# RMS norm on one core: three loads moved to ScalarE's DMA queue, the last tile's halves swapped

## Chip, core and metric

The kernel runs on one core of one Trainium2 chip. The metric is device time in microseconds (us), the median of several runs. One further execution was taken with the hardware profiler; all rows and instants below come from it, counted from the start of its span. A "unit" below is half a tile, 4096 KB of data.

## What is computed

The input x has 16 x 1024 rows of 512 float32 numbers. Each row is divided by its root mean square and multiplied by a vector gamma of 512 numbers:

```python
rms = np.sqrt(np.mean(x ** 2, axis=-1, keepdims=True) + 1e-5)
return (x / rms * gamma).astype(np.float32)
```

33.6 MB are read and 33.6 MB written. Nothing is reused between rows but gamma.

## The kernel before

The 16384 rows are four tiles of 4096. In a tile each of the 128 partitions holds 32 whole rows, so half a tile (16 rows per partition) is 32 KB per partition and 4096 KB in all. On the chip there are three buffers, `slots[0]` to `slots[2]` (line 40), each of one tile. Tiles 0, 1 and 2 have a slot each; tile 3 reuses slot 0 (`slot_of`, line 86), so its loads must wait until tile 0 has been stored. Rows 23 to 31 of slot 2 also serve as scratch for tile 0's squares (line 90), so that part of tile 2 can't be loaded before VectorE has read those squares.

The work goes group by group, a group being half a tile (`groups`, lines 76 to 85: tile, first row, number of rows, the pieces in which the squares are taken, and how many rows GpSimd scales). For a group:

- `square_sums` (line 88): ScalarE squares a piece (line 95), VectorE sums it by row (line 96). Pieces alternate between one PSUM buffer of 7 rows and one SBUF buffer of 5 rows, so a third piece waits until VectorE has read the first.
- `inverse_rms` (line 100): ScalarE's square root (line 101), VectorE's reciprocal (line 102).
- GpSimd scales its share of the rows and multiplies them by gamma (lines 108, 109). ScalarE scales the others, one instruction per row (line 117), and VectorE multiplies them by gamma (line 121).

The loop at line 161 is a software pipeline: in the turn of one group ScalarE squares the next group's first two pieces, scales the first half of its rows of this group, squares the third piece, and scales the second half. Every engine executes its own instructions in the order written; nothing reorders them (`manual_schedule`, line 33).

All DMAs are issued by SyncE (SP) and stand in one queue, q1. SP issues in the order written and waits, before an issue, for what that transfer depends on. The order is: tile 0 in three loads with gamma between them, both halves of tile 1, and then what `transfers` (line 128) adds: both halves of tile 2, both stores of tile 0, both loads of tile 3 (each waits until the store of the same rows has landed), one store of the whole of tile 1, one of tile 2, and two stores of tile 3, first half first. SP issues the last store when VectorE has done line 121 of the last group.

In the text below, L2b is the load of tile 2's second half, S0a the store of tile 0's first half, and so on; L1 and S1 are of a whole tile.

Of the kernel before, what the change touches and what calls it, by code (L numbers as in the profile page):

```python
# [9 lines left out]
def kernel(  # L10
# [6 lines left out]
    nc = tc.nc  # L17
# [12 lines left out]
    xv = xf.rearrange("(t p r) d -> t p r d", p=P, r=R)  # L30
# [9 lines left out]
    slots = [const.tile([P, R, D], fp32, name=f"slot{i}") for i in range(3)]  # L40

    before_scale = []

    def load(t, slot, r0, r1):
        dma = nc.sync.dma_start(out=slots[slot][:, r0:r1], in_=xv[t][:, r0:r1])  # L45
        before_scale.append((slot, r0, r1, dma))

    def store(t, slot, r0, r1):
        dma = nc.sync.dma_start(out=ov[t][:, r0:r1], in_=slots[slot][:, r0:r1])
        before_scale.append((slot, r0, r1, dma))  # L50

    gamma_row = const.tile([1, D], fp32)
    pieces = (0, D)

    load(0, 0, 0, 1)
    load(0, 0, 1, 16)
    for c0, c1 in zip(pieces, pieces[1:]):
        nc.sync.dma_start(out=gamma_row[:, c0:c1], in_=gamma.unsqueeze(0)[:, c0:c1])
    load(0, 0, 16, 32)
    load(1, 1, 0, 16)  # L60
    load(1, 1, 16, 32)

    ones_col = const.tile([1, P], fp32)
    nc.gpsimd.memset(ones_col, 1.0)  # L64
# [15 lines left out]
        (1, 16, 16, (7, 5, 4), 7),  # L80
        (2, 0, 16, (7, 5, 4), 7),
        (2, 16, 16, (7, 5, 4), 7),
        (3, 0, 16, (7, 5, 4), 7),
        (3, 16, 16, (7, 5, 4), 3),
    ]
    slot_of = [0, 1, 2, 0]

    def square_sums(ss, t, g, r, m, k):
        if m == 9:
            sq = slots[2][:, 23:32, :]  # L90
        else:
            home, name, most = ((psum, "sq_psum", 7), (const, "sq_sbuf", 5))[k % 2]
            sq = home.tile([P, most, D], fp32, name=name)
        rows = slots[slot_of[t]][:, g + r : g + r + m, :]
        nc.scalar.activation(out=sq[:, :m], in_=rows, func=AF.Square)  # L95
        nc.vector.tensor_reduce(  # L96
            out=ss[:, r : r + m, 0], in_=sq[:, :m], axis=mybir.AxisListType.X, op=OP.add
        )

    def inverse_rms(ss, n):  # L100
        nc.scalar.activation(out=ss[:, :n, 0], in_=ss[:, :n, 0], func=AF.Sqrt, bias=eps_t, scale=1.0 / D)  # L101
        nc.vector.reciprocal(out=ss[:, :n, 0], in_=ss[:, :n, 0])  # L102
        return ss

    def scale_by_pool(rstd, t, g, n, share):
        part = slots[slot_of[t]][:, g + n - share : g + n, :]
        by_row = rstd[:, n - share : n].to_broadcast([P, share, D])
        nc.gpsimd.tensor_tensor(out=part, in0=part, in1=by_row, op=OP.mult)  # L108
        last = nc.gpsimd.tensor_tensor(  # L109
            out=part, in0=part, in1=gamma_b.to_broadcast([P, share, D]), op=OP.mult  # L110
        )
        before_scale.append((slot_of[t], g + n - share, g + n, last))

    def scale(rstd, t, g, r0, r1):
        x = slots[slot_of[t]]
        for r in range(r0, r1):
            nc.scalar.activation(out=x[:, g + r, :], in_=x[:, g + r, :], func=AF.Copy, scale=rstd[:, r])  # L117

    def times_gamma(t, g, r0, r1):
        part = slots[slot_of[t]][:, g + r0 : g + r1, :]  # L120
        scaled = nc.vector.tensor_tensor(  # L121
            out=part, in0=part, in1=gamma_psum.to_broadcast([P, r1 - r0, D]), op=OP.mult
        )
        for slot, b0, b1, earlier in before_scale:
            if slot == slot_of[t] and b0 < g + r1 and g + r0 < b1:
                tc.declare_no_dep(scaled.ins, earlier.ins, reason="ScalarE waited for it before it scaled these rows")

    def transfers(t, g):
        if (t, g) == (0, 0):
            load(2, 2, 0, 16)  # L130
            load(2, 2, 16, 32)
        elif (t, g) == (0, 16):
            store(0, 0, 0, 16)
            store(0, 0, 16, 32)
            load(3, 0, 0, 16)
            load(3, 0, 16, 32)
        elif (t, g) == (1, 16):
            store(1, 1, 0, 32)
        elif (t, g) == (2, 16):
            store(2, 2, 0, 32)  # L140
        elif (t, g) == (3, 0):
            store(3, 0, 0, 16)
        elif (t, g) == (3, 16):
            store(3, 0, 16, 32)

    def pieces_of(group):
        t, g, n, pieces, share = group
        ss = stats.tile([P, 16, 1], fp32, name="ss")
        r = 0
        todo = []  # L150
        for k, m in enumerate(pieces):
            todo.append((ss, t, g, r, m, k))
            r += m
        return ss, todo
# [6 lines left out]
    for k, group in enumerate(groups):  # L161
        t, g, n, pieces, share = group
        mine = n - share
        half = (mine + 1) // 2
        ahead = groups[k + 1 :][:1]
        ss, todo = pieces_of(ahead[0]) if ahead else (None, [])
        scale_by_pool(rstd, t, g, n, share)
        for piece in todo[:2]:
            square_sums(*piece)
        scale(rstd, t, g, 0, half)  # L170
        for piece in todo[2:]:
            square_sums(*piece)
        scale(rstd, t, g, half, mine)
        times_gamma(t, g, 0, mine)
        transfers(t, g)
        for nxt in ahead:
            rstd = inverse_rms(ss, nxt[2])

# [29 lines left out]
```

## Time and profile before

| what | us |
|---|---|
| median of 3 runs (161.77 to 162.13) | 161.85 |
| the profiled execution's own time | 161.72 |
| its span | 159.9 |
| VectorE (DVE) busy | 112.8 |
| ScalarE (ACT) busy | 109.1 |
| GpSimd (POOL) busy | 102.1 |
| DMA queue q1, share of 16 engines' span | 98.1% |

The span begins with the first instruction and ends with the last. The rows show when an instruction started and how long it took, and for a DMA the time from its issue to its landing, which is when its semaphore is complete. A DMA's issue instant plus its time to landing gives the instant from which others may use the data. The queue takes transfers in order, so the time to landing holds the time that a transfer stood behind others.

### The profile page before, as it was taken

The page shows a single profiled execution, that of the slowest core. Times are in us where ns is not written, and L with a number is a line of the kernel's source. Part 1 is how long each engine was busy: PE and PEld are TensorE (multiplying, and loading weights), DVE is VectorE, ACT ScalarE, POOL GpSimd, SP SyncE. Part 2 cuts the span into 40 slices and gives each one's busy share as a digit, 9 for nine tenths or more (in the row PEclk, how much of TensorE's full clock was granted, in tenths as well). Part 3 has the DMA queues.
Part 4 walks back from the last instruction along what each step waited for, and adds up shares of the span by engine and source line. Part 5 has one row for each costly group of instructions (what it writes and reads, how often), then busy time and mean ns, then how long its engine had stood idle before and what let it go on. Part 6 is the DMA issues. An engine that isn't in the chain of part 4 may idle for free.

```text
span 159.9 us, 258 instructions
## 1 busy us (share of the span) xinstructions
PE 2.0 (1%) x2; PEld 0.5 (0%) x2; DVE 112.8 (71%) x38; ACT 109.1 (68%) x110; POOL 102.1 (64%) x22
## 2 busy tenths in 40 slices
PE   0005000000000000000000000000000000000000
PEld 0001000000000000000000000000000000000000
DVE  0000993797999999999999999999999702950000
ACT  3007906999998899899989989999994297000000
POOL 1000005994079999999999999999999997000000
DMA  5989999999999997999999999997997998999995
GB/s 191 492 369 468 451 393 434 484 393 418 484 410 393 483 426 311 483 393 402 508 402 393 492 426 393 524 475 311 524 459 328 524 426 361 393 459 459 393 426 229
DMA packets 2163, 67.12 MB, mean 420 GB/s; under 512 B 241, under 2 KB 241, under 8 KB 370
## 3 DMA queue, kind: packets, MB, share of 16 engines
q1 hardware_dynamic: 2162, 67.11, 98.1%
q14 instruction: 1, 0.01, 0.0%
HBM read 33.56 MB, written 33.55 MB: 420 GB/s over the span
## 4 chain that ended last, share of the span: by engine, by line
DVE 62%; ACT 18%; DMA 7%; ACTq 0%; SPq 0%; issue 0%
DVE ss L96 36%; DVE slot L121 26%; ACT slot L117 9%; DMA slot<-in_x_dram 7%; ACT slot L95 5%; ACT sq_psum L95 4%; DVE ss L102 1%; ACTq L203 0%; ACT gamma_b L160 0%; SPq L45 0%; ACT ss L101 0%; ACTq L95 0%
## 5 line engine op out<-in xcount | busy, mean ns | idle before, releaser
L108 POOL TENSOR_TENSOR slot<-slot,ss 128x3584 f32<-128x3584 f32 (+2 forms) x8 | 45.0, 5625 | 31.8 <-DVE ss L102 31.8
L96 DVE TENSOR_REDUCE ss<-sq_psum 128x7 f32<-128x3584 f32 (+1 forms) x14 | 44.5, 3176 | 19.5 <-ACT sq_psum L95 19.5
L109 POOL TENSOR_TENSOR slot<-slot,gamma_b 128x3584 f32<-128x3584 f32 (+2 forms) x8 | 56.9, 7112 | 0.6
L117 ACT ACTIVATE slot<-slot,ss 128x512 f32<-128x512 f32 x77 | 48.5, 707 | 4.9 <-DVE ss L102 4.9
L121 DVE TENSOR_TENSOR slot<-slot,gamma_psum 128x4608 f32<-128x4608 f32 (+2 forms) x8 | 42.3, 5282 | 9.3 <-ACT slot L117 9.3
L95 ACT ACTIVATE sq_psum<-slot 128x3584 f32<-128x3584 f32 (+1 forms) x14 | 36.5, 2604 | 11.4 <-DMA slot<-in_x_dram 10.4
L96 DVE TENSOR_REDUCE ss<-sq_sbuf 128x5 f32<-128x2560 f32 x6 | 16.8, 2806 | 0.0
L95 ACT ACTIVATE sq_sbuf<-slot 128x2560 f32<-128x2560 f32 x6 | 13.9, 2320 | 0.0
L96 DVE TENSOR_REDUCE ss<-slot 128x9 f32<-128x4608 f32 x2 | 9.9, 4953 | 0.1
L101 ACT ACTIVATE ss<-ss,eps_t 128x16 f32<-128x16 f32 x8 | 2.4, 306 | 8.4 <-DVE ss L96 8.4
L95 ACT ACTIVATE slot<-slot 128x4608 f32<-128x4608 f32 x2 | 8.1, 4028 | 0.0
L102 DVE RECIPROCAL ss<-ss 128x16 f32<-128x16 f32 x8 | 2.0, 249 | 0.4 <-ACT ss L101 0.4
L66 PE MATMUL gamma_psum<-gamma_row,ones_col 1*128 1x512 f32 x2 | 2.0, 1120 | 12.8 <-DMA gamma_row<-in_gamma_dram 12.8
L72 ACT ACT_TABLE_LOAD x1 | 1.3, 1283 | 1.1 <-PEq L192 1.1
L160 ACT COPY gamma_b<-gamma_psum 128x512 f32<-128x512 f32 x1 | 0.6, 566 | 0.0
L66 PEld LDWEIGHTS gamma_psum<-gamma_row,ones_col 1*128 1x128 f32 x2 | 0.5, 304 | 12.8 <-issue 12.8
L64 POOL MEMSET ones_col<- 1x128 f32 x1 | 0.2, 194 | 0.3 <-POOLq L192 0.3
L192 POOL MEMSET const-float32-0.0<- 128x1 f32 x1 | 0.1, 98 | 0.2 <-issue 0.2
L72 ACT ACTIVATE table<-eps_t 128x1 f32<-128x1 f32 x1 | 0.2, 203 | 0.0
L192 POOL MEMSET const-bfloat16-1.0<- 128x1 bf16 x1 | 0.1, 101 | 0.0
L192 POOL MEMSET const-uint8-127<- 128x1 uint8 x1 | 0.1, 101 | 0.0
L192 POOL MEMSET const-float32-1.0<- 128x1 f32 x1 | 0.1, 98 | 0.0
(1 smaller groups left out, 0.1 us busy)
## 6 DMA issues: line engine op xcount, KB each, us to landing
slot<-in_x_dram SPq DMA_DIRECT2D x7, 4096.0 KB, 27.1
out_dram<-slot SPq DMA_DIRECT2D x4, 4096.0 KB, 21.8
slot<-in_x_dram SPq DMA_DIRECT2D x1, 3840.0 KB, 11.8
slot<-in_x_dram SPq DMA_DIRECT2D x1, 256.0 KB, 3.1
out_dram<-slot SPq DMA_DIRECT2D x2, 29.2
gamma_row<-in_gamma_dram SPq DMA_DIRECT2D x1, 2.0 KB
```

The costliest lines, as they stand in the source:

```text
L66: nc.tensor.matmul(gamma_psum[:, 0], ones_col, gamma_row, start=True, stop=True)
L72: nc.scalar.activation(out=table, in_=eps_t, func=AF.Sqrt)
L95: nc.scalar.activation(out=sq[:, :m], in_=rows, func=AF.Square)
L96: nc.vector.tensor_reduce(out=ss[:, r : r + m, 0], in_=sq[:, :m], axis=mybir.AxisListType.X, op=OP.add)
L101: nc.scalar.activation(out=ss[:, :n, 0], in_=ss[:, :n, 0], func=AF.Sqrt, bias=eps_t, scale=1.0 / D)
L102: nc.vector.reciprocal(out=ss[:, :n, 0], in_=ss[:, :n, 0])
L108: nc.gpsimd.tensor_tensor(out=part, in0=part, in1=by_row, op=OP.mult)
L109: last = nc.gpsimd.tensor_tensor(out=part, in0=part, in1=gamma_b.to_broadcast([P, share, D]), op=OP.mult)
L117: nc.scalar.activation(out=x[:, g + r, :], in_=x[:, g + r, :], func=AF.Copy, scale=rstd[:, r])
L121: scaled = nc.vector.tensor_tensor(out=part, in0=part, in1=gamma_psum.to_broadcast([P, r1 - r0, D]), op=OP.mult)
L160: nc.scalar.copy(out=gamma_b[:, 0], in_=gamma_psum[:, 0])
L192: nc = _bacc.Bacc("TRN2", target_bir_lowering=False, num_devices=1)
```

## The change

Transfers only; every computing instruction stays, and on VectorE, GpSimd and TensorE the order and the shapes stay too. On ScalarE three DMA issues are put between the computing instructions.

1. L1 becomes one load of 8192 KB (before: two of 4096 KB). L2a follows at once.
2. L2b, L3b and L3a are issued by ScalarE, on a queue of its own: L2b in the turn of group (0, 16) after the first scaling; L3b in the turn of (1, 16) after the third piece of squares; L3a in the turn of (2, 0) after the first two pieces of squares.
3. The last two groups change places: (3, 16) with GpSimd's share 7 comes first, (3, 0) with share 3 last.
4. S0b is issued before S0a. S1 becomes S1a and S1b, and S1a is made to wait until L3b has landed. S3b is issued before S3a.

```diff
-    load(1, 1, 0, 16)
-    load(1, 1, 16, 32)
+    load(1, 1, 0, 32)
+    load(2, 2, 0, 16)
...
-        (3, 0, 16, (7, 5, 4), 7),
-        (3, 16, 16, (7, 5, 4), 3),
+        (3, 16, 16, (7, 5, 4), 7),
+        (3, 0, 16, (7, 5, 4), 3),
...
-    def transfers(t, g):
-        if (t, g) == (0, 0):
-            load(2, 2, 0, 16)
-            load(2, 2, 16, 32)
-        elif (t, g) == (0, 16):
+    late = {}
+
+    def loads_amid(t, g, step):
+        if (t, g, step) == (0, 16, 1):
+            load(2, 2, 16, 32, queue=nc.scalar)
+        elif (t, g, step) == (1, 16, 2):
+            late[3] = load(3, 0, 16, 32, queue=nc.scalar)
+        elif (t, g, step) == (2, 0, 0):
+            load(3, 0, 0, 16, queue=nc.scalar)
+
+    def stores(t, g):
+        if (t, g) == (0, 16):
+            store(0, 0, 16, 32)
             store(0, 0, 0, 16)
-            store(0, 0, 16, 32)
-            load(3, 0, 0, 16)
-            load(3, 0, 16, 32)
         elif (t, g) == (1, 16):
-            store(1, 1, 0, 32)
+            store(1, 1, 0, 16, behind=late[3])
+            store(1, 1, 16, 32)
         elif (t, g) == (2, 16):
             store(2, 2, 0, 32)
-        elif (t, g) == (3, 0):
-            store(3, 0, 0, 16)
-        elif (t, g) == (3, 16):
-            store(3, 0, 16, 32)
+        elif t == 3:
+            store(3, 0, g, g + 16)
...
         for piece in todo[:2]:
             square_sums(*piece)
+        loads_amid(t, g, 0)
         scale(rstd, t, g, 0, half)
+        loads_amid(t, g, 1)
         for piece in todo[2:]:
             square_sums(*piece)
+        loads_amid(t, g, 2)
         scale(rstd, t, g, half, mine)
         times_gamma(t, g, 0, mine)
-        transfers(t, g)
+        stores(t, g)
```

`load` takes the queue as an argument; `store` takes `behind`, a load whose landing the issue waits for.

More of the change, by code (lines that the diff above doesn't have):

```diff
@@ L42, with load, store @@
     before_scale = []
-    def load(t, slot, r0, r1):
-        dma = nc.sync.dma_start(out=slots[slot][:, r0:r1], in_=xv[t][:, r0:r1])
+    def load(t, slot, r0, r1, queue=nc.sync):
+        dma = queue.dma_start(out=slots[slot][:, r0:r1], in_=xv[t][:, r0:r1])
         before_scale.append((slot, r0, r1, dma))
-    def store(t, slot, r0, r1):
+        return dma
+    def store(t, slot, r0, r1, behind=None):
         dma = nc.sync.dma_start(out=ov[t][:, r0:r1], in_=slots[slot][:, r0:r1])
+        if behind is not None:
+            tc.add_manual_dep(
+                dma.ins,
+                behind.ins.name,
+                mybir.DependencyInfo(mybir.DependencyClass.Sync, mybir.DependencyReason.DATA),
+                reason="the store is issued when this load has landed",
+            )
         before_scale.append((slot, r0, r1, dma))
```

## Prediction

> **What bounds the kernel now.** I read the busy shares first, then the DMA queue, then the chain of waits, then the last rows of the timeline. From the page:
>
> ```profile
> DMA  5989999999999997999999999997997998999995
> GB/s 191 492 369 468 451 393 434 484 393 418 484 410 393 483 426 311 483 393 402 508 402 393 492 426 393 524 475 311 524 459 328 524 426 361 393 459 459 393 426 229
> ...
> q1 hardware_dynamic: 2162, 67.11, 98.1%
> ...
> DVE 62%; ACT 18%; DMA 7%; ACTq 0%; SPq 0%; issue 0%
> ```
>
> The chain says VectorE, and misleads: it starts from the last computing instruction and leaves out the DMA behind it. That instruction is the second row here, from the timeline; the first is the last store's issue, from SyncE's timeline:
>
> ```profile
> 142.22 0.33 SPq L49 DMA_DIRECT2D out_dram<-slot  x1
> ...
> 135.06 7.09 DVE L121 TENSOR_TENSOR slot<-slot,gamma_psum 128x6656 f32<-128x6656 f32 x1 [8.13 <-ACT slot L117]
> ```
>
> VectorE ends at 142.15, the span at 159.9. Between them lies only storing, and the last store takes 16.9 us from issue to landing though a unit (4096 KB) needs 9.7: it stood behind S3a. These are the DMA issues, each asked for in a short window: L2a (issued at 3.40), L2b (38.01), L3b (81.97), S1 (86.93), S3b (142.22):
>
> ```profile
> slot<-in_x_dram SPq DMA_DIRECT2D x1, 4096.0 KB, 48.4
> ...
> slot<-in_x_dram SPq DMA_DIRECT2D x1, 4096.0 KB, 24.2
> ...
> slot<-in_x_dram SPq DMA_DIRECT2D x1, 4096.0 KB, 19.1
> ...
> out_dram<-slot SPq DMA_DIRECT2D x1, 33.5
> ...
> out_dram<-slot SPq DMA_DIRECT2D x1, 4096.0 KB, 16.9
> ```
>
> Issue plus time gives landings. The loads issued at 1.17, 2.02, 2.40, 2.89, 3.40 and 38.01 landed at 12.97, 22.7, 32.4, 42.1, 51.8 and 62.2: **9.7 us a unit**, but 10.4 for the last. L3b landed at 101.1, S1 (two units) at 120.4, S3b at 159.1. From 12.97 fifteen units follow: 12.97 + 15 x 9.71 = 158.6. So in the whole run the queue lost 0.5 us, all of it around 60 us, where loads hand over to stores. The windows say the same: 434 GB/s where only loads run, 320 in the 4 us around the handover, 431 where only stores run:
>
> ```profile
> 13.00:42.00 29.00, 1.88 (x2) 0.30 (x2) 20.79 (x6) 23.93 (x18) 12.01 (x2) 1.00 1.01 434
> ...
> 60.00:64.00 4.00, 0.00 (x0) 0.00 (x0) 4.00 (x2) 3.91 (x5) 4.00 (x1) 1.00 0.75 320
> ...
> 144.00:158.00 14.00, 0.00 (x0) 0.00 (x0) 0.00 (x0) 0.00 (x0) 0.00 (x0) 1.00 1.00 431
> ```
>
> The kernel is bound by the bytes that 16 DMA engines move. The change moves the same bytes. It can win at most the 0.6 us at the handover, unless two queues together run faster than one; it can lose by leaving the engines dry or by making them alternate.
>
> **SyncE's waits taken away: 0.** SyncE stood 22.2 us in front of L3a and L3b, waiting for S0a and S0b to land. Behind it stood only S1, whose data were ready at 86.93, and the engines were busy throughout.
>
> **L1 in one load.** Its semaphore now comes with the whole tile, at 42.1. ScalarE's next squares ran from 39.23 on, since L1a had landed at 32.4. The rows that move:
>
> ```profile
> 39.23 3.14 ACT L95 ACTIVATE sq_psum<-slot 128x3584 f32<-128x3584 f32 x1
> ...
> 44.72 3.83 DVE L96 TENSOR_REDUCE ss<-sq_psum 128x7 f32<-128x3584 f32 x1
> ...
> 48.58 1.88 ACT L95 ACTIVATE sq_psum<-slot 128x2048 f32<-128x2048 f32 x1 [0.57 <-DVE ss L96]
> ...
> 53.38 4.95 DVE L121 TENSOR_TENSOR slot<-slot,gamma_psum 128x4608 f32<-128x4608 f32 x1
> ```
>
> ScalarE: 42.2 + 3.14 + 2.32 (second piece) + 3.17 (five scalings) = 50.8, then L2b's issue. Such a row exists on SyncE only, 0.33 to 0.47; I take 0.35 (bounds 0 and 0.5): 51.1. Third piece to 53.0, four scalings to 55.5. Line 121 starts at 55.5 instead of 53.38: VectorE's chain is **2.1 us late**, and stays so, as VectorE has no idle time from 39 to 127. GpSimd's next share waits for the reciprocal, 60.4 instead of 58.88, thus 1.5 late. The two later issues cost nothing: ScalarE idles 0.56 per turn at line 101.
>
> What covers this: the last store would be issued at 142.22 + 2.1 = 144.3, while S3b holds the engines until about 149.0. A first byte follows an issue by 0.8 to 1.3 us (the first issue is at 0.74, the first bytes are in the slice 1.5 to 2.0). So 3.4 us or more of cover are left, and the direct price is 0. With no cover it would be 2.1.
>
> **First handover to stores.** SyncE now issues S0b first, which needs line 121 of group (0, 16): ready at 58.33 before, at 60.4 after. S0a, ready at 44.7, stands behind it. Meanwhile only L2b feeds the engines, on ScalarE's queue: issued at 50.8, in time, as L2a lands at 51.8. Without a handover L2b would land at 51.8 + 9.7 = 61.5, its last bytes some 0.4 earlier (L0's bytes end and landing stand about so). S0b's first bytes come at 60.4 + 0.8 to 1.3 = 61.2 to 61.7. Gap: 0.1 to 0.6, and the old loss of 0.6 may be gone (the queue is another) or come on top. Against the 0.6 of before: -0.5 to +0.6. I take +0.1, a gap of 0.35 with half of the old loss.
>
> The Trainium skill, "DMA: Bandwidth & Descriptors", section "Latency and other measured facts", gives about 0.6 us to the first byte for queues of SyncE and ScalarE. By it this gap would be 0 and the sum 0.3 lower; the row here, 0.8 or more, is longer, and I go by the row.
>
> **Second handover, S0a to L3b.** ScalarE reaches L3b's issue at 77.8 + 2.1 = 79.9, first bytes at 80.7 to 81.2. S0b and S0a, begun at 61.5, end at 61.5 + 19.4 = 80.9. Gap 0 to 0.3; I take 0.1. The issue itself waits for S0b, landed by about 72; nothing waits on ScalarE. L3a's issue at 88.5 waits for S0a, landed by 82.
>
> **Two queues at once.** L3b lands at about 91.2, only then is S1a issued, with S1b behind it. L3a has been running since 90.8 on the other queue. From 92.4 both have work: 6.6/8 of a unit of L3a is left, and if both get half, the mixed stretch lasts 2 x 0.83 x 9.7 = 16 us, to 108.5. No row shows two queues. Nearest rows: loads alone and stores alone run at 434 and 431 GB/s, so a mean of them costs 0; a handover inside one queue cost 0.6 once and 0 once (L3b to S1: 120.4 - 101.1 = 19.3 for two units of 9.7). A unit is 128 blocks of 32 KB (one per partition) for 16 engines, eight each; seven changes at 0.6 would be 4 us. The lower end: the window 100 to 120 shows 462 GB/s, 6% over, though its neighbour 419, since large packets are counted at their end; 6% of 16 us would be -1.0. I take +0.2, near the row of 0.
>
> L3a lands at about 109.0 (needed by the squares of group (3, 0) at 108.46 + 2.1 = 110.6). The margin is 1.6 us.
>
> That both get half is supported by the same page, section "Queues, rings and completion order", which says that each engine goes round-robin between queues, packet by packet. By it L3a is in time; no row of this trace can show it.
>
> **The rest.** S1a and S1b end with L3a's bytes at 90.8 + 3 x 9.7 = 119.9; S2, issued at 114.93 + 1.5 = 116.4, follows without a gap; S3b is ready at 128.9 + 1.5 = 130.4, S2's bytes last to 139.3. Swapping the halves of tile 3 changes no duration: the shapes stay.
>
> **Sum:** 161.72 (profiled execution: span 159.9 and 1.82 around it) + 0.1 + 0.1 + 0.2 = **162.1 us**. The median of the runs is 0.13 above that execution, too little to correct for. A measurement of this kernel can tell about 0.2%, 0.3 us, from no change: "within 0.2%" is 161.5 to 162.2.
>
> **Rivals.**
> - *Same floor, small gaps (my forecast)*: 161.5 to 162.2. For it: 98.1% busy, 0.5 us lost in all, equal bytes. Chance 0.40.
> - *Alternating costs*: engines that switch between a load and a store lose part of 0.6 us at each of the seven or so changes, 0.1 to 0.3 each: +0.7 to +2, so 162.4 to 163.7, likeliest 162.9. For it: the row of 320 GB/s. Against: L3b to S1 at no loss. Chance 0.24. Both gaps at their long ends (+0.6, +0.3) give 162.6: 0.06.
> - *L3a starved, the other side*: if SyncE's queue gets two turns of three, L3a's 0.83 units take 3 x 0.83 x 9.7 = 24 us, to 116.6, landing at 117.1. ScalarE's squares wait 6.5 us, the last store is issued at 150.8, first bytes at 151.8 against S3b's end at 149.2: a dry gap of 2.6, so 164.7. It decides from a landing of L3a later than about 114.3; before that the cover of 3.4 to 4 us swallows it. Chance 0.08.
> - *The loss at 60 us goes*: the first handover without loss and a gap of 0.1 gives -0.5, the second one 0: 161.2. For it: it's the one hole in the queue. Against: S0b's bytes come later than before. Chance 0.16.
> - *Loads and stores overlap in two queues*: -1.0 and the above, 160.7. Only the 462 speaks for it. Chance 0.06.
> - *The change does nothing it says*: excluded for the order (ScalarE has the three issues in its sequence); its intent, that nothing waits, fails if ScalarE stands at L3b's issue, 8 us away from that.
>
> **Numbers.** Faster 0.16 + 0.06 = 0.22, same 0.40, slower 0.24 + 0.06 + 0.08 = 0.38. The range 160.9 to 163.8 leaves out the starved case, and the ends of alternating and of overlap, under 0.2 together. The forecast's own range is 161.5 to 162.2.
>
> **What would show it.** Right: two hardware queues near 98% together; ScalarE waiting 2.9 us for a load at line 103 before 42.2; VectorE's last instruction ending near 144.3; the last landing within 0.5 of 159.1. Handovers: windows of 60 to 64 and 79 to 83 below 430 GB/s. Alternating: the rate from 92 to 108 well below 430. Starved: ScalarE waiting for a load after 110. The forecast is wrong if the rate with two queues differs by over 2% from that of one, or if VectorE's last instruction ends after 148.

## The result: 162.8 us, 0.6% slower

The kernel after takes 162.81 us in the median of six runs (162.5 to 163.1), the kernel before beside it 161.84. The ratio is 1.0056, 95% interval 1.0041 to 1.0071. The profiled execution took 162.78 (before: 161.72), its span is 160.8 (159.9).

From the page of the kernel after, the lines that answer to those of before: DMA share and rate in 40 slices, the queues, the chain of waits.

```profile
DMA  6989999969999999999999999999996996999993
GB/s 205 474 367 497 416 391 522 522 261 522 391 391 489 424 391 391 489 416 399 391 391 505 408 383 399 391 514 399 391 636 277 522 505 277 391 505 408 391 481 171
...
q1 hardware_dynamic: 1730, 54.53, 79.4%
q10 hardware_dynamic: 432, 12.58, 18.6%
...
DVE 50%; DMA 25%; ACT 13%; SPq 1%; ACTq 0%; issue 0%
```

ScalarE's queue is q10. Both queues together fill 79.4 + 18.6 = 98.0% of the span: the engines are as full as before, with the same bytes, in a longer span. So a part of the busy time is slow time. The timeline of the kernel after shows that nothing else became the bound:

```profile
42.06 3.16 ACT L103 ACTIVATE sq_psum<-slot 128x3584 f32<-128x3584 f32 x1 [2.73 <-DMA slot<-in_x_dram]
...
44.86 0.38 ACTq L45 DMA_DIRECT2D slot<-in_x_dram  x1
...
54.82 4.96 DVE L129 TENSOR_TENSOR slot<-slot,gamma_psum 128x4608 f32<-128x4608 f32 x1 [0.19 <-ACT slot L125]
...
136.50 7.09 DVE L129 TENSOR_TENSOR slot<-slot,gamma_psum 128x6656 f32<-128x6656 f32 x1 [8.13 <-ACT slot L125]
143.66 0.33 SPq L50 DMA_DIRECT2D out_dram<-slot  x1
```

ScalarE waits 2.73 us for L1; VectorE ends 1.4 us later than before, at 143.6; the last store is issued at 143.66, still behind S3b. These are the DMA issues of the kernel after, one row each (kind, queue, KB, us to landing): L2b (issued at 44.86), S0b (59.85), S0a (60.30), L3b (77.46), L3a (82.32), S1b (91.99), S2 (116.08), S3a (143.66).

```profile
slot<-in_x_dram ACTq DMA_DIRECT2D x1, 4096.0 KB, 16.6
...
out_dram<-slot SPq DMA_DIRECT2D x1, 4096.0 KB, 12.0
...
out_dram<-slot SPq DMA_DIRECT2D x1, 4096.0 KB, 21.3
...
slot<-in_x_dram ACTq DMA_DIRECT2D x1, 4096.0 KB, 14.0
...
slot<-in_x_dram ACTq DMA_DIRECT2D x1, 4096.0 KB, 25.6
...
out_dram<-slot SPq DMA_DIRECT2D x1, 4096.0 KB, 29.3
...
out_dram<-slot SPq DMA_DIRECT2D x1, 24.5
...
out_dram<-slot SPq DMA_DIRECT2D x1, 4096.0 KB, 16.3
```

They landed at 61.5, 71.9, 81.6, 91.5, 107.9, 121.3, 140.6 and 160.0. At 9.71 us a unit, S0b lost 0.7, L3b 0.1 to 0.2, and the three units from L3b to S1b (29.8 for 29.1) 0.7. From S1b on nothing is lost: the difference stands at 121.3 and is carried to the end (before: S1 at 120.4, last landing 159.1). The windows of the kernel after show where in the last 0.7 the time went (last column GB/s):

```profile
92.00:97.00 5.00, 0.00 (x0) 0.00 (x0) 5.00 (x3) 4.44 (x7) 4.92 (x2) 1.00 0.95 354
97.00:108.00 11.00, 0.00 (x0) 0.00 (x0) 11.00 (x5) 10.91 (x11) 11.00 (x2) 1.00 0.99 429
```

The rate falls when S1a joins L3a, and then, while the two take turns, it is 429, what one queue reaches. The loss is at the start of the meeting, not in the turns.

A landing comes with the slowest of the 16 engines; a rate is that of all of them. These are the windows around the first change of direction (loads to stores) and the second (stores to loads), of the kernel before and then of the kernel after:

```profile
57.00:64.00 7.00, 0.00 (x0) 0.00 (x0) 7.00 (x4) 6.91 (x7) 7.00 (x2) 1.00 1.01 384
77.00:84.00 7.00, 0.00 (x0) 0.00 (x0) 7.00 (x3) 6.44 (x7) 6.92 (x2) 1.00 1.04 449
...
57.00:64.00 7.00, 0.00 (x0) 0.00 (x0) 7.00 (x4) 6.64 (x8) 5.92 (x2) 1.00 0.99 417
77.00:84.00 7.00, 0.00 (x0) 0.00 (x0) 7.00 (x4) 6.35 (x8) 6.92 (x2) 1.00 0.99 384
```

Before, the first change is dear and the second is free; after, it is the other way round. The trace also has every single block (the 32 KB of one partition's 16 rows) with its start and duration. A block takes 1.21 us in both kernels, but at these changes up to 2.04 us before and 2.10 us after. If each block's bytes are spread over its own duration and 4096 KB are worth 9.71 us, the 16 engines together lost, in us:

| stretch | before | after |
|---|---|---|
| 57 to 64 (first change) | 0.87 | 0.28 |
| 77 to 84 (second change) | 0 | 0.69 |
| 91 to 104 (loads of tile 3 to S1) | 0.09 | 0.65 |

So all engines together lost 0.7 more than before; the rest of the 0.8 by which the last landing is later is the slowest engine's. At the first two changes together the engines lost about the same in both kernels (0.87 and 0.97). If the blocks are chained, each one put on the engine whose last block has just ended, every engine of the kernel after lost 0.8 to 1.1 us at these two, most of them nearly all of it at one of the two. A few paid at the first, and S0b landed 0.7 late with the slowest of them; the others paid at the second. The new loss is that of the third stretch.

### The profile page after: what moved, and what is told of

Read it like the earlier page. It is cut to its first block, busy times and chain, and to the rows that moved or that the text cites. A ratio compares the mean times of both kernels' runs of the same rounds, so it can differ in the third digit from the quotient of the medians.

```text
span 160.8 us, 256 instructions
## 1 busy us (share of the span) xinstructions
PE 2.0 (1%) x2; PEld 0.5 (0%) x2; DVE 113.1 (70%) x38; ACT 108.9 (68%) x110; POOL 102.2 (64%) x22
## 3 DMA queue, kind: packets, MB, share of 16 engines
q1 hardware_dynamic: 1730, 54.53, 79.4%
q10 hardware_dynamic: 432, 12.58, 18.6%
## 4 chain that ended last, share of the span: by engine, by line
DVE 50%; DMA 25%; ACT 13%; SPq 1%; ACTq 0%; issue 0%
DVE ss L104 27%; DMA slot<-in_x_dram 25%; DVE slot L129 23%; ACT slot L125 8%; ACT sq_psum L103 3%; ACT sq_sbuf L103 1%; SPq L45 1%; DVE ss L110 1%; ACTq L218 0%; SPq L66 0%; ACTq L45 0%
```

## The experiments

A **hole** below is a stretch of some 2 us in which the rate falls though the engines stay busy, that is, in which blocks take longer. The kernel before has one, at its first change from loads to stores. My first theory after the result was "newcomer": a hole comes where work of the other direction has only just been issued, mostly on a second queue. Rivals: "direction" (every change costs) and "count" (a fixed place in the queue).

**e1, one load more.**

```diff
-    load(0, 0, 16, 32)
+    load(0, 0, 16, 24)
+    load(0, 0, 24, 32)
```

> The kernel before with the load of tile 0's second half in two loads of 2048 KB. The same bytes, one more DMA, so that each engine takes nine more queue entries ahead of tile 1. Theory 'count': the hole near 60 us of the kernel before (0.6 us) belongs to the 62nd to 64th entry that an engine takes from q1, which the kernel after reaches where its own hole at 79 us lies; then the hole moves to where L2a hands over to L2b, near 51 to 53 us, and the windows 60 to 64 show 430 GB/s. Theories 'direction' (each change from loads to stores or back costs 0.6) and 'newcomer' (a hole where work of the other direction has only just been issued): it stays at 60. The time is 161.8 within 0.3 by all.

Measured: 161.89, ratio 0.9995 (0.9985 to 1.0005). The hole stays (57 to 64 us: 398 GB/s). "Count" falls.

**e2, S0b issued later.**

```diff
         elif (t, g) == (0, 16):
             store(0, 0, 0, 16)
+        elif (t, g) == (1, 0):
-            store(0, 0, 16, 32)
+            store(0, 0, 16, 32, behind=sums[1, 16, 0])
             load(3, 0, 0, 16)
             load(3, 0, 16, 32)
```

> The kernel before, but S0b is issued only when VectorE has summed the first piece of group (1, 16), near 62.3 us, and not at 58.95 in the middle of the handover from L2b to S0a; S0a, issued at 44.7, keeps the engines busy until 71. Theory 'newcomer': the hole at 60 came from S0b's issue, so it shrinks to the 0.1 of the handover from L3b to S1, and the time falls by 0.5 to 161.3. Theories 'direction' and 'count': the hole stays, 161.8.

Measured: 161.80, ratio 0.9996 (0.9987 to 1.0005). S0b was issued at 62.31 and the hole stayed (375 GB/s): against "newcomer".

**e3, the kernel after on one queue.**

```diff
-            load(2, 2, 16, 32, queue=nc.scalar)
+            load(2, 2, 16, 32)
...
-            late[3] = load(3, 0, 16, 32, queue=nc.scalar)
-        elif (t, g, step) == (2, 0, 0):
-            load(3, 0, 0, 16, queue=nc.scalar)
+            late[3] = load(3, 0, 16, 32)
+            load(3, 0, 0, 16)
...
-            store(1, 1, 0, 16, behind=late[3])
+            store(1, 1, 0, 16)
```

> The kernel after with all transfers on SyncE's queue: L2b right behind L2a, L3b and L3a behind S0a and ahead of S1a. Order of tiles, halves and shapes as in the kernel after. Theory 'newcomer': the holes at 79 and 94 us go, as work of the other direction has then stood in the queue for some time; the hole at the first handover stays: 161.9. Theory 'direction': the same three changes of direction still cost 0.6 each: 162.8.

Measured: 163.00, ratio 1.0066 (1.0051 to 1.0081). All of the loss is there without a second queue, as "direction" had it: "newcomer" falls, and so does the second queue as a needed cause.

**e4, the second queue alone.**

```diff
+        if (t, g, step) == (1, 16, 2):
+            late[3] = load(3, 0, 0, 16, queue=nc.scalar)
+        elif (t, g, step) == (2, 0, 0):
+            load(3, 0, 16, 32, queue=nc.scalar)
...
-            load(3, 0, 0, 16)
-            load(3, 0, 16, 32)
...
-            store(1, 1, 0, 32)
+            store(1, 1, 0, 16, behind=late[3])
+            store(1, 1, 16, 32)
```

> The kernel before with one part of the change alone: L3a and L3b on ScalarE's queue at the change's two places, and S1 in halves, the first of them issued when L3a has landed. L1 in two loads, L2b on SyncE's queue, the order of halves as before. If the second queue alone makes the loss ('newcomer' and 'direction' both): two new holes of 0.6 at 79 and 94 us beside the old one at 60, 162.8 to 163.0. Rival, that L1 in one load and S0b first make it: 161.9.

Measured: 161.98, ratio 1.0006 (0.9996 to 1.0015). A second queue on which loads meet stores costs nothing that can be told. Windows of e4 around its first two changes of direction:

```profile
57.00:64.00 7.00, 0.00 (x0) 0.00 (x0) 7.00 (x4) 6.91 (x7) 7.00 (x2) 1.00 0.98 365
77.00:84.00 7.00, 0.00 (x0) 0.00 (x0) 7.00 (x3) 6.44 (x7) 6.92 (x2) 1.00 1.04 449
```

The old hole and no second one, although L3a comes by the other queue while S0b is still running; and where S1a joins L3b the rate is 433 (92 to 97 us). The two new holes that were expected from the second queue did not come. So neither "newcomer" nor "direction". What after and e3 share, and e4 does not, is the order of halves and L1 in one load. I tried the order, and with it whether addresses decide.

**e5, the order of halves alone.**

```diff
-        (3, 0, 16, (7, 5, 4), 7),
-        (3, 16, 16, (7, 5, 4), 3),
+        (3, 16, 16, (7, 5, 4), 7),
+        (3, 0, 16, (7, 5, 4), 3),
...
-            store(0, 0, 0, 16)
             store(0, 0, 16, 32)
-            load(3, 0, 0, 16)
+            store(0, 0, 0, 16)
             load(3, 0, 16, 32)
+            load(3, 0, 0, 16)
```

> The kernel before with the order of halves alone changed: S0b ahead of S0a, L3b ahead of L3a, group (3, 16) ahead of (3, 0). One queue, L1 in two loads, S1 whole. Theory 'halves' (which halves meet at a change of direction decides, neither the queue nor the freshness of the work): holes of 0.6 to 0.9 at the handovers S0a to L3b near 79 us and L3a to S1 near 97 us, the time 162.7 to 163.0. Rival 'load in one piece' (L1 in one load, or S1 in halves, makes the holes, as the two kernels with holes, after and one queue, share these too): no hole at 79 and 97, 161.9.

Measured: 162.80, ratio 1.0057 (1.0033 to 1.0081), single runs from 161.91 to 163.43 (before beside it: 161.64 to 162.19). This edit alone makes a loss of the change's size in the median, though two of its ten runs (161.91 and 161.93) show none. Windows of e5:

```profile
57.00:64.00 7.00, 0.00 (x0) 0.00 (x0) 7.00 (x4) 6.91 (x7) 7.00 (x2) 1.00 1.00 431
77.00:84.00 7.00, 0.00 (x0) 0.00 (x0) 7.00 (x3) 6.44 (x7) 6.92 (x2) 1.00 0.99 407
```

The other way round than in e4: the first change is free, the second is not. By the landings the next, L3a to S1, is dearest: L3a was issued at 81.48, after S0a's landing, took 20.5, and so landed 20.5 us behind S0a, for two units of 19.4.

**e6 and e7, HBM rows exchanged** in tiles 0 and 3, in the kernel after (e6) and in the kernel before (e7).

```diff
+    def hbm(view, t, r0, r1):
+        h = 0 if t not in (0, 3) else 16 if r0 < 16 else -16
+        return view[t][:, r0 + h : r1 + h]
...
-in_=xv[t][:, r0:r1]
+in_=hbm(xv, t, r0, r1)
...
-out=ov[t][:, r0:r1]
+out=hbm(ov, t, r0, r1)
```

> The kernel after, but for tiles 0 and 3 the on-chip rows 0 to 15 of the slot take the HBM rows 16 to 31 of each partition and the other way round, in loads and stores alike; every transfer keeps its place in the order, its issue, its slot rows and its size. Only the HBM addresses that meet are exchanged. Theory 'HBM': the holes at 79 and 94 follow the HBM rows and go, 161.9. Rival 'slot' (the on-chip rows or the instant decide): the holes stay, 162.8.

> The kernel before with the same exchange of HBM rows in tiles 0 and 3. Theory 'HBM': holes of 0.6 or more appear at the handovers S0b to L3a (81 us) and L3b to S1 (99 us), as in the kernel after, and the first handover (60 us) changes as well, its hole falling to about 0.2: 162.3 to 162.9. Rival 'slot': as before, 161.9, one hole at 60.

Measured: e6 163.04, ratio 1.0079 (1.0064 to 1.0094), holes as in after (77 to 84 us: 384 GB/s). e7 161.85, ratio 1.0004 (0.9995 to 1.0014), holes as in before. "HBM" falls.

**e8, the same exchange in tile 2 alone**, in the kernel before, with S2 in two halves.

```diff
-        h = 0 if t not in (0, 3) else 16 if r0 < 16 else -16
+        h = 0 if t not in (2,) else 16 if r0 < 16 else -16
...
-            store(2, 2, 0, 32)
+            store(2, 2, 0, 16)
+            store(2, 2, 16, 32)
```

> The kernel before with the HBM rows exchanged in tile 2 alone (S2 in halves for that). The work that meets at the first handover is then tile 2's first HBM half with tile 0's first. Theory 'HBM': the hole at 60 changes; if it goes, the time is 161.2, under both kernels. Rival 'slot': the hole at 60 stays, 161.9.

Measured: 162.00, ratio 1.0013 (1.0003 to 1.0022). The hole at the first change stays (57 to 64 us: 370 GB/s). Whether the 0.13% comes from the exchange or from S2 in two halves was not tried.

Two things were left of the order of halves: which rows of slot 0 meet, or when the first store is issued. In the kernel before S0a is issued at 44.7. With the halves exchanged SyncE stands before S0b until 59 to 60, and S0a, ready since 44.7, waits behind it.

**e9, upper halves first throughout**: the change's order of slot rows, with the early store.

```diff
-    load(0, 0, 0, 1)
-    load(0, 0, 1, 16)
+    load(0, 0, 16, 17)
+    load(0, 0, 17, 32)
...
-        (0, 0, 16, (7, 9), 6),
-        (0, 16, 16, (7, 9), 7),
+        (0, 16, 16, (7, 9), 6),
+        (0, 0, 16, (7, 9), 7),
...
-        elif (t, g) == (0, 16):
-            store(0, 0, 0, 16)
+        elif (t, g) == (0, 0):
             store(0, 0, 16, 32)
+            store(0, 0, 0, 16)
```

(The second load of tile 0 and the halves of tile 3 change places as well.)

> The kernel before with tiles 0 and 3 worked second half first throughout: loaded, computed and stored so. The order of halves in slot 0 at the changes of direction is that of the kernel after (S0b, S0a, L3b, L3a), but the first store is issued at 44.7 as in the kernel before, 16 us before the loads ahead of it end. Theory 'slot' (which rows of the slot meet at a change of direction decides): holes as in the run with the order of halves alone changed, 0.5 at S0a to L3b and 1.0 at L3a to S1, 162.8. Theory 'early store' (the first store, issued long before the loads run out, pays 0.6 at 60 us once, and later changes of direction are then nearly free): as the kernel before, 161.85, one hole at 60.

Measured: 161.72, before beside it 161.72, ratio 0.9996 (0.9987 to 1.0006). "Slot" falls. Windows of e9, first and second change of direction:

```profile
57.00:64.00 7.00, 0.00 (x0) 0.00 (x0) 7.00 (x4) 6.91 (x7) 7.00 (x2) 1.00 0.97 351
77.00:84.00 7.00, 0.00 (x0) 0.00 (x0) 7.00 (x3) 6.44 (x7) 6.92 (x2) 1.00 1.04 449
```

**e10, a late first store** in the order of the kernel before.

```diff
-            store(0, 0, 0, 16)
+            store(0, 0, 0, 16, behind=done[0, 16])
             store(0, 0, 16, 32)
```

> The kernel before, but S0a is issued only when VectorE has multiplied the rows of group (0, 16) by gamma, at 58.4 and not at 44.7, with S0b at 58.95 behind it; the order of halves and slots stays that of the kernel before. L2b ends at 61, so the engines don't run dry. Theory 'early store': the first handover loses nothing (as when the order of halves alone was changed: 9.67 for S0b's unit) and the later ones S0b to L3a and L3b to S1 lose 0.5 and 0.7 to 1.0: 162.4 to 162.9, with a wide spread. Theory 'slot': as before, 161.85, one hole at 60.

Measured: 162.19, under the 162.4 to 162.9 of "early store" and over the 161.85 of "slot"; ratio 1.0033 (1.0016 to 1.0050), runs from 161.87 to 162.96. Four of the ten runs (161.87 to 161.94) lie among those of the kernel before beside them (161.61 to 162.0). In the profiled execution (162.41) S0a was issued at 58.32; L2b landed at 61.5 and S0a at 71.2, both on time, S0b lost 0.3, and then L3b (issued at 81.22, just after S0b's landing, 20.5 to landing) lost 1.1 of two units. This one edit, a wait in front of one store, moves the hole from the first change to the later ones, as e5 does; it costs time in some runs and not in others. Windows of e10:

```profile
57.00:64.00 7.00, 0.00 (x0) 0.00 (x0) 7.00 (x4) 6.91 (x7) 7.00 (x2) 1.00 0.99 426
77.00:84.00 7.00, 0.00 (x0) 0.00 (x0) 7.00 (x3) 6.44 (x7) 6.92 (x2) 1.00 1.01 421
```

**e11, the kernel after with the order of halves undone.**

```diff
-        (3, 16, 16, (7, 5, 4), 7),
-        (3, 0, 16, (7, 5, 4), 3),
+        (3, 0, 16, (7, 5, 4), 7),
+        (3, 16, 16, (7, 5, 4), 3),
...
-            late[3] = load(3, 0, 16, 32, queue=nc.scalar)
+            late[3] = load(3, 0, 0, 16, queue=nc.scalar)
...
-            load(3, 0, 0, 16, queue=nc.scalar)
+            load(3, 0, 16, 32, queue=nc.scalar)
...
-            store(0, 0, 16, 32)
             store(0, 0, 0, 16)
+            store(0, 0, 16, 32)
```

> The kernel after with one part undone: S0a ahead of S0b, so that it is issued at 44.7 when its rows are ready; with it L3a ahead of L3b and group (3, 0) ahead of (3, 16). ScalarE's queue for L2b, L3a and L3b, L1 in one load, S1 in halves behind the first load of tile 3: all as in the kernel after. Theory 'early store': the holes at 79 and 94 go; the first handover, now S0a taking turns with L2b from about 51 on, pays 0.6 once: 161.9. If taking turns spares that too: 161.2. Rival, that L1 in one load or L2b's queue have a share in the loss: 162.3 to 162.8.

Measured: 162.51, ratio 1.0043 (1.0028 to 1.0058). The hole at 79 goes (77 to 84 us: 449 GB/s), but the first one moves forward and grows: S0a now joins L2b, and the window 51 to 56 of e11 shows

```profile
51.00:56.00 5.00, 0.00 (x0) 0.00 (x0) 4.33 (x3) 5.00 (x7) 4.92 (x2) 1.00 1.05 360
```

From L1's landing to S0a's, three units, it takes 1.0 too long, against 0.6 to 0.7 before, and 0.2 to 0.3 more go from there to S1b. The 161.9 of "early store" did not come; the time lies in the range of the rival, that L1 in one load or L2b's queue has a share in the loss (162.3 to 162.8). The interval of e11 overlaps with that of after, so it isn't even shown that the order of halves matters in the kernel after. At most a part of its loss can be the late store's.

**e12, the first store on ScalarE's queue**, meant as the best version.

```diff
-            store(0, 0, 0, 16)
             store(0, 0, 16, 32)
...
+        if (t, g) == (0, 16):
+            store(0, 0, 0, 16, queue=nc.scalar)
         scale(rstd, t, g, 0, half)
```

> The kernel before with S0a alone issued by ScalarE on its own queue at about 44.8, ahead of its scaling of group (0, 16); all else on SyncE's queue. S0a then takes turns with L2a and L2b from about 48 on and does not stand behind them. If the 0.6 us of the first handover is the price of a sudden change from loads to stores, it goes, and later changes stay free, as the store came early: 161.2, the best of all. If it is paid once by the first store in whatever manner: 161.85. If later changes cost again: 162.2 or more.

Measured: 161.65, before beside it 161.75, ratio 0.9998 (0.9987 to 1.0008), runs from 161.45 to 162.12. In the profiled execution the hole isn't spared, only moved: S0a meets L2a at 47, and the window 46 to 50 shows 360 GB/s. (That execution took 162.10, among the slowest of the ten.) No version faster than the kernel before was found.

The runs side by side, rates in GB/s from the windows, S1's landing (all of it) as issue plus time to landing:

| kernel | first store issued | 57 to 64 us | 77 to 84 us | S1 landed | median | ratio |
|---|---|---|---|---|---|---|
| before | 44.7 | 384 | 449 | 120.4 | 161.8 | |
| e4 second queue alone | 44.8 | 365 | 449 | 120.4 | 161.98 | 1.0006 |
| e9 upper first | 44.6 | 351 | 449 | 120.7 | 161.72 | 0.9996 |
| e10 late store | 58.3 | 426 | 421 | 121.2 | 162.19 | 1.0033 |
| e5 order of halves | 59.0 | 431 | 407 | 121.4 | 162.80 | 1.0057 |
| e3 one queue | 59.8 | 421 | 375 | 121.6 | 163.00 | 1.0066 |
| after | 59.9 | 417 | 384 | 121.3 | 162.81 | 1.0056 |
| e11 order undone | 44.8 | 431 (hole at 51 to 56) | 449 | 121.0 | 162.51 | 1.0043 |
| e12 store on q10 | 44.8 | 426 (hole at 46 to 50) | 445 | 120.8 | 161.65 | 0.9998 |

449 is over the 432 of a full queue (4096 KB in 9.71 us) because a block of 32 KB or 64 KB is counted whole in the window in which it starts, and not at its end as the prediction has it; the column serves to compare kernels.

The rates hide one difference. For each store the trace has sixteen signals, one about 0.35 us after the last block of each of the 16 engines, and a store has landed with the last of them. For the last store of each profiled execution, in us:

| kernel | mean of the sixteen | last one |
|---|---|---|
| before | 158.85 | 159.12 |
| e10 late store | 158.72 | 159.79 |
| e5 order of halves | 158.96 | 160.04 |
| e11 order undone | 159.18 | 159.67 |
| after | 159.52 | 159.94 |
| e3 one queue | 159.87 | 160.18 |

In e10 and e5 the engines together are about where they are in the kernel before; but one lags 1.1 us behind the mean, from the landing of tile 3's second load at 102 us on, and every later store waits for it. That fits runs of which some show no loss, though only one execution of each kernel was traced. In after and in e3 all sixteen are late by 0.7 to 1.0. So e5 makes a loss of the change's size, but not the same loss: what the kernel after and e3 share beside the order of halves, L1 in one load above all, may have a part in it.

## Why the prediction was right and wrong

The measured time lies in the range of 160.9 to 163.8, 0.4% above the forecast and outside the forecast's own range of 161.5 to 162.2. It is in the "slower" that had 0.38, behind "same" with 0.40. Two of the signs set down in advance went against the forecast: the last landing moved by 0.9, not within 0.5, and with both queues at work from 92 to 108 the rate was 406 GB/s, over 2% below the 434 and 431 of one.

- **Bound by the engines that move bytes**: right. The last landing moved by 0.9 (159.1 to 160.0), the median by 0.97, and no computing engine waits for anything new that matters.
- **L1 in one load**: the wait is there, 2.73 us, forecast 2.9. VectorE's chain came 1.4 us late, forecast 2.1; half of the difference is the DMA issue on ScalarE, taken at 0.35, which took nothing of its time: it went out at 44.86, before the computing instructions that stand ahead of it had started. The direct price was 0 as said: the last store still stood behind S3b.
- **The two handovers**: +0.1 each forecast, as gaps without bytes beside half of the old loss. No gap came: S0b was issued at 59.85, before L2b landed at 61.5, and L3b at 77.46, before S0a landed at 81.6. By the landings both look right (S0b lost 0.7 where 0.6 to 0.7 was lost before; L3b 0.1 to 0.2). But a landing is the slowest engine's. All engines together lost 0.28 instead of 0.87 at the first handover and 0.69 instead of 0 at the second. The sum, +0.1 for +0.2 forecast, is right; the two places are not, and that they cancel was no part of the forecast.
- **Two queues at once: the step that failed**, "I take +0.2, near the row of 0". The engines together lost 0.65 there, against 0.09 in the kernel before (by the landings 0.7, of which 0.5 is the miss in the sum). The size was off, and the mechanism too: I priced turns between the queues, and turns are free (429 GB/s from 97 to 108); the price is paid once where S1a meets L3a (354 from 92 to 97). And it isn't a price of two queues: e4 has them and loses nothing, e3 has one and loses all.
- **The rest of the sum**: 0.4 forecast, 1.06 measured in the profiled executions (161.72 to 162.78): 0.9 in the span, and 0.16 around it, 1.98 us instead of 1.82.
- **The rival "alternating costs"** named 162.4 to 163.7 and 162.9 as likeliest. Its time came true, and so did its sign, a rate from 92 to 108 well below 430; its mechanism, a loss at each of seven turns, did not.
- **What I treated as harmless**: "S0a, ready at 44.7, stands behind it." I saw that the early store goes and gave it no price, since the engines weren't dry. e10 shows that this alone moves the hole to the later changes and costs 0.33% in the median; e5 that the order of halves as a whole costs 0.57%. I read the one hole of 0.6 in the kernel before as a price of that handover, and its absence at the later two as their nature. In e5, e10 and the kernel after, the later ones were not free where the first one was cheap.
- **Starved L3a**: it landed at 107.9, forecast 109.0, and its squares ran at 109.9 without waiting. The Trainium skill, "DMA: Bandwidth & Descriptors", section "Queues, rings and completion order", has each engine go round-robin between its queues. The trace agrees: from 97 to 106 us each engine took blocks of the two queues in turn, one by one.

**What stays open.** Shown is: the loss lies in slow blocks at changes of direction; neither the second queue, nor HBM rows, nor slot rows are needed for it; in the traces of e5 and e10 a late first store goes with a free first change and dear later ones. Not shown is what in an engine carries this from 60 to 97 us, why in e5 and e10 one engine lags while in after and e3 all are late, and why e11, with the early store, keeps most of the loss. L1 in one load and L2b's queue were not tried alone, so the cause of the loss in the kernel after itself stays open in part. Each kernel was traced in one execution only.

## What to carry to other kernels

When the queue is full for 98% of the span, the wait lists and the chain say little: issue plus time to landing for each transfer, against the time of a unit, shows where the engines lose, and how much there is to win at most (here 0.5 us). A landing tells of the slowest engine only; put the rate beside it before you charge a loss to one place. A change in the order of loads and stores can cost at places where no engine is idle. Holding back a store that was ready early cost 0.33% here (e10), so don't put it behind one that is ready later without a reason; giving the early store back to the kernel after (e11) isn't shown to win anything. A hole that appears once in a profile is no price list: what follows it in the same run may be cheap because of it, as e5 and e10 suggest.

## What the runs showed of the hardware

- Where loads and stores meet on full engines, a hole appears once or more per run. A block of 32 KB, 1.21 us elsewhere, takes up to 2.04 us there (before), 2.10 (after), 2.31 (e3), and the engines together lose 0.2 to 1.1 us at one change, with the DMA share at 0.95 or more in the windows of 4 to 7 us around it that stand above. Some changes cost nothing (e4, e9: the second one, 449 GB/s). Taking turns afterwards runs at 429 GB/s, as one direction does (434 and 431).
- A store lands with its slowest engine: in e5 and e10 one engine lagged by 1.1 us behind the mean of sixteen, in the kernel before the last one lagged by 0.27.
- Two kernels with a late first store spread more: 161.87 to 162.96 (e10) and 161.91 to 163.43 (e5), against 161.61 to 162.0 and 161.64 to 162.19 for the kernel before beside them. The kernel after (162.5 to 163.1) and e3 (162.8 to 163.07), whose first store is as late, do not.
- A DMA issue in ScalarE's sequence goes out before earlier computing instructions of that engine have started: L2b's at 44.86, with squares at 45.15 and five scalings from 47.38 ahead of it in the order. It took no time from ScalarE's work: the squares at 45.15 follow those begun at 42.06 (3.16 us) without a gap.
